# Up products of a SwiGLU trunk made token by token, with eleven pairs of weight pieces multiplied in seven quarter products instead of eight

## The chip, the core and the metric

The kernel runs on one core of a Trainium2 chip. The engines are named as in the profile: PE multiplies matrices (PEld is its loading of the stationary operand), DVE and ACT work element by element, POOL does small work on statistics, and SP issues the DMA transfers. The metric is the device time of one execution in microseconds (us); the median of several runs is compared.

## What is computed

Two layers of a decoder trunk for 256 tokens of 1024 features, everything in float32. Each layer is a half-step SwiGLU, a token mixer beside a memory attention, and a second half-step SwiGLU:

```python
def swiglu(h, w_up, w_down):
    gate, up = jnp.split(h @ w_up, 2, axis=-1)
    return (jax.nn.silu(gate) * up) @ w_down

x = x + 0.5 * swiglu(rmsnorm(x, norm_g[i, 0]), ffn_w_up[i, 0], ffn_w_down[i, 0])
h = rmsnorm(x, norm_g[i, 1])
# mixer: multi-scale causal pooling in layer 0, differential attention in layer 1
x = x + mix
x = x + 0.5 * swiglu(rmsnorm(x, norm_g[i, 2]), ffn_w_up[i, 1], ffn_w_down[i, 1])
```

The change lies in the four SwiGLUs. `w_up` is 1024 x 5632 (gate and up of 2816 each), `w_down` is 2816 x 1024.

## The kernel before, in words

**Float32 in two parts.** Every operand of a product is split exactly into two float32r parts, hi and lo. ACT makes hi by a cast, DVE makes lo by a subtraction, and a product is hi·hi + hi·lo + lo·hi, added up in PSUM. The weights stream from HBM in pieces of 128 x 2048 numbers (1 MB). One DMA on SP loads a piece into one of three raw buffers, four casts and four subtractions of 512 columns split it (L196 to L210), and at most four split pieces are alive (`WB = 4`); a fifth waits until PE has read the oldest.

**One SwiGLU.** `ffn` (L401) goes over eleven column blocks j. A block's up weights are two pieces (upper and lower half of the 1024 rows, each with 256 gate and 256 up columns), its down weights are one piece.
- The first block (three in the first SwiGLU) is made *token by token*: `proj_tok` (L344) keeps 128 tokens stationary and streams 512 weight columns, three matmuls of 512 columns (`mm3`, L230) for each of eight K tiles. Then `gated` takes silu on ACT and the product with the up half on DVE, and PE transposes the result, since the down product needs features on the partitions.
- The other blocks are made *wide*, feature by feature: `proj_wide` (L368) keeps 128 x 128 weights stationary and streams the hi and lo columns of all tokens side by side, one matmul of 512 columns and one of 256 for each K tile. Nothing has to be transposed. ACT and DVE add the two halves of the bank, multiply by the row of token norms, take silu and multiply.
- The down product of a block (`accumulate`, L387) adds 24 matmuls of 512 columns to four PSUM banks.

At the end of a SwiGLU or a mixer, `close` (L293) transposes the new x on PE, and ACT and DVE write its columns, times the gain, into `xT` as hi and lo. The norm of a token (`rstd`) is made meanwhile on ACT and POOL, and comes in only after the up product.

**What sets the order.** `Flow` (L63) writes the instructions of PE, ACT, DVE and SP in an order that it plans by hand-set spacings: products form the main stream, and the steps of chains (split a piece, gate a block, close a tile) are laid between them. Each engine then works strictly down its list: an instruction that waits holds all that stand behind it.

## Time and profile before

| | |
|---|---|
| median of 3 runs | 1035.28 us (1034.5 to 1036.14) |
| span of the profiled execution | 1033.5 us |
| PE busy | 99% of the span |
| DVE busy | 72% |
| ACT busy | 59% |
| granted clock of PE | 0.998 on the mean |

The profile page gives the busy time of each engine, the span in 40 slices, the chain of work that ended last, and the costliest groups of instructions. In a row of a group, "418" is the mean time of one in ns; the start of the next one can lie before the reported end of the last, since the engines are pipelined. The span goes from the first to the last instruction; the 1.8 us that the median is longer lie around it.

### The profile page before, as it was taken

How to read it: one execution, taken by the hardware profiler on the slowest of the kernel's cores; microseconds unless marked ns; L12 is line 12 of the kernel's file. 1: busy time of each engine (PE TensorE's matmuls, PEld its weight loads, DVE VectorE, ACT ScalarE, POOL GpSimd, SP SyncE). 2: the span in 40 equal slices, each digit the busy share in tenths (PEclk: the TensorE clock that was granted, in tenths of full speed). 3: DMA queues.
4: the chain of work that ended last, by engine and by line, in shares of the span. 5: the costliest groups of instructions: out<-in, count | busy, mean ns of one | idle time of the engine just before them, and what ended most of it. 6: DMA issues, size and time to landing. Idle time of an engine off the chain costs nothing.

```text
span 1033.5 us, 15028 instructions
## 1 busy us (share of the span) xinstructions
PE 1022.4 (99%) x5624; PEld 882.0 (85%) x5624; DVE 739.6 (72%) x1533; ACT 610.4 (59%) x1357; POOL 55.8 (5%) x125
## 2 busy tenths in 40 slices
PE   8999999999999999999999999999999999999997
PEld 7888888899888888888888888889998888888886
DVE  5767887756767677777777777756877867777675
ACT  5655755765666555556655565654766666555553
POOL 0000520100000000000000000010211000000000
PEclk9999999999999999999999999999999999999999
DMA  8754745535544555544554545446334544455541
GB/s 300 286 189 163 267 181 204 201 130 188 182 140 168 192 199 193 200 170 163 204 202 165 204 163 204 169 157 237 120 134 142 185 158 168 164 203 178 195 178 41
DMA packets 27993, 188.31 MB, mean 182 GB/s; under 512 B 3216, under 2 KB 3472, under 8 KB 5904
## 3 DMA queue, kind: packets, MB, share of 16 engines
q1 hardware_dynamic: 27632, 186.82, 49.7%
q8 instruction: 44, 0.72, 0.3%
q10 hardware_dynamic: 288, 0.52, 0.1%
q14 instruction: 29, 0.24, 0.1%
HBM read 186.29 MB, written 1.05 MB: 181 GB/s over the span
## 4 chain that ended last, share of the span: by engine, by line
PE 95%; DVE 2%; ACT 1%; DMA 1%; POOL 0%; SPq 0%; issue 0%; POOLq 0%; ACTq 0%
PE mm L377 28%; PE mm L379 12%; PE acc L231 10%; PE acc L233 10%; PE acc L232 10%; PE mm L231 6%; PE mm L233 6%; PE mm L232 6%; PE mm L376 2%; PE tr L237 1%; DMA raw<-in_ffn_w_up 1%; DVE lo L208 1%; ACT ds L841 1%; PE acc L822 0%; PE tr L232 0%; PE tr L233 0%
## 5 line engine op out<-in xcount | busy, mean ns | idle before, releaser
L208 DVE TENSOR_TENSOR lo<-raw,hi 128x512 fp32r<-128x512 f32 x684 | 440.7, 688 | 43.0 <-ACT hi L205 42.7
L377 PE MATMUL mm<-xT,hi 128*128 128x512 f32 x1216 | 424.2, 398 | 0.0
L205 ACT CAST hi<-raw 128x512 fp32r<-128x512 f32 x684 | 385.1, 618 | 26.9 <-PE mm L232 14.2
L379 PE MATMUL mm<-xT,lo 128*128 128x256 f32 x1064 | 298.5, 281 | 0.0
L377 PEld LDWEIGHTS mm<-xT,hi 128*128 128x128 f32 x1216 | 220.8, 188 | 42.4
L379 PEld LDWEIGHTS mm<-xT,lo 128*128 128x128 f32 x1064 | 201.0, 189 | 6.4
L231 PE MATMUL acc<-hi,gh 128*128 128x512 f32 x352 | 138.1, 392 | 0.0
L233 PE MATMUL acc<-hi,gl 128*128 128x512 f32 x352 | 137.1, 389 | 0.0
L232 PE MATMUL acc<-lo,gh 128*128 128x512 f32 x352 | 137.0, 389 | 0.0
L385 DVE TENSOR_TENSOR g<-g,mm 128x256 f32<-128x256 f32 x76 | 32.0, 421 | 80.6 <-ACT g L384 80.4
L384 ACT COPY s<-mm 128x256 f32<-128x256 f32 x76 | 28.3, 372 | 98.7 <-PE mm L377 98.7
L232 PEld LDWEIGHTS acc<-lo,gh 128*128 128x128 f32 x352 | 66.2, 188 | 13.9
L233 PEld LDWEIGHTS acc<-hi,gl 128*128 128x128 f32 x352 | 66.1, 188 | 14.0
L231 PEld LDWEIGHTS acc<-hi,gh 128*128 128x128 f32 x352 | 66.1, 188 | 11.9
L385 DVE TENSOR_TENSOR s<-s,mm 128x256 f32<-128x256 f32 x76 | 31.9, 420 | 57.8 <-ACT s L384 57.7
L439 ACT ACTIVATE s<-s 128x256 f32<-128x256 f32 x76 | 31.8, 418 | 68.5 <-DVE s L437 68.5
L220 ACT CAST gh<-g 128x256 fp32r<-128x256 f32 x76 | 30.9, 407 | 65.8 <-DVE g L445 65.8
L231 PE MATMUL mm<-xT,hi 128*128 128x256 f32 x192 | 55.9, 291 | 0.0
L233 PE MATMUL mm<-xT,lo 128*128 128x256 f32 x192 | 54.5, 284 | 0.0
L232 PE MATMUL mm<-xT,hi 128*128 128x256 f32 x192 | 54.3, 283 | 0.0
L231 PE MATMUL mm<-hi,xT 128*128 128x512 f32 x128 | 50.9, 398 | 0.0
L233 PE MATMUL mm<-hi,xT 128*128 128x512 f32 x128 | 50.0, 390 | 0.0
(190 smaller groups left out, 1364.1 us busy)
## 6 DMA issues: line engine op xcount, KB each, us to landing
raw<-in_ffn_w_up SPq DMA_DIRECT2D x86, 1024.0 KB, 4.8
raw<-in_ffn_w_down SPq DMA_DIRECT2D x44, 1024.0 KB, 5.0
raw<-in_diff_w_in SPq DMA_DIRECT2D x14, 1024.0 KB, 4.8
raw<-in_mem_w_kv SPq DMA_DIRECT2D x8, 1024.0 KB, 4.8
raw<-in_pool_w_in SPq DMA_DIRECT2D x6, 1024.0 KB, 4.9
raw<-in_pool_w_out SPq DMA_DIRECT2D x6, 1024.0 KB, 4.8
raw<-in_diff_w_out SPq DMA_DIRECT2D x6, 1024.0 KB, 4.7
raw<-in_ffn_w_up SPq DMA_DIRECT2D x8, 256.0 KB, 7.0
```

Source lines behind the costliest of these rows:

```text
L205: nc.scalar.copy(hi[:, sl], raw[:, sl])
L208: nc.vector.tensor_sub(lo[:, sl], raw[:, sl], hi[:, sl].bitcast(F32))
L220: nc.scalar.copy(hi, src)
L231: nc.tensor.matmul(o, lh, rh, start=start, stop=False)
L232: nc.tensor.matmul(o, lh, rl, start=False, stop=False)
L233: nc.tensor.matmul(o, ll, rh, start=False, stop=stop)
L376: nc.tensor.matmul(o[:, 0:SEQ], wl, hx[0][:, kk, :], start=False, stop=False)
L377: nc.tensor.matmul(o, wh, hx[2][:, kk, :], start=kk == 0, stop=last)
L379: nc.tensor.matmul(o[:, 0:SEQ], wl, hx[0][:, kk, :], start=False, stop=False)
L384: nc.scalar.copy(out, o[:, SEQ:2 * SEQ])
L385: nc.vector.tensor_add(out, out, o[:, 0:SEQ])
L439: nc.scalar.activation(s, s, AF.Silu)
```

## The change

All blocks of a SwiGLU are made token by token; `proj_wide` and its helpers are gone. Up blocks are either *single* (as `proj_tok` before) or taken in *pairs* of two blocks, two pairs in the first SwiGLU and three in each of the others. A pair is a product of a 2 x 2 matrix of operand quarters (two tiles of 128 tokens, two halves of K) and a 2 x 2 matrix of weight pieces (two halves of K, two blocks): eight quarter products before, seven now. Each quarter product is four `mm3`, twelve matmuls of 512 columns. They are made in the order 1, 5, 6, then the down product of an earlier block, then 2, 7, 3, 4.

For this the pair needs sums. Of the weights: piece 5 is b11 + b12, piece 6 adds b22 to that, piece 4 is b21 plus all the others, and piece 7 is b12 + b22. (The signs of the scheme sit in the sums of the operand and in the order of subtraction.) DVE makes these in float32 in place in the raw buffers, eight additions of 128 x 1024, and all seven pieces are split into hi and lo. Pieces b12 and b22 are loaded into the room of the mixers' tiles (`qk`, `mq`). Of the operand: `column_sums`, once for each SwiGLU, multiplies the float32 columns by the row of norms and makes five sums of 128 x 512, each split.

The seven results are put together by DVE (`less`, `gate_sum`): u2 = result 6 − m1 where m1 is result 1 copied out by ACT, then product 7 is added to the same bank and u3 = that − m1, u2 += result 3, u3 += m5, c21 = m1 − result 4. Each of the four quarters is then gated (silu on ACT, product on DVE) and transposed on PE, two transposes for each quarter and block.

Other edits: a split works in halves of 1024 columns instead of quarters of 512; `close` first writes the scaled columns in float32 and then casts them, four activations and one cast on ACT and one subtraction on DVE where there were four and four; the weight queue counts free buffers by kind; the condition that queues the memory's columns and statistics in the first SwiGLU now holds at two of its steps, so that they are loaded and made twice.

```diff
-SPLIT = 512
+SPLIT = 1024
+PAIR = (0.15, 0.9, 0.55, 0.75)
+PAIR_SLACK = 3.0
...
     def split_piece(key, raw, before):
...
+        for s in range(0, PIECE, SPLIT):
+            sl = slice(s, s + SPLIT)
+            if before is not None:
+                nc.vector.tensor_add(raw[:, sl], raw[:, sl], before[:, sl])
+            nc.scalar.copy(hi[:, sl], raw[:, sl])
+            yield pace
+        for s in range(0, PIECE, SPLIT):
+            sl = slice(s, s + SPLIT)
+            nc.vector.tensor_sub(lo[:, sl], raw[:, sl], hi[:, sl].bitcast(F32))
...
     def close(t, gain0, xg):
...
+            for k in range(4):
+                g = gain0 + 4 * h + k
+                nc.scalar.activation(c[:, k, :], b[h][:, cols(k)], AF.Copy, scale=gcol[:, g:g + 1])
+            b[h] = c
+            split_hi(xT[0][:, 4 * h:4 * h + 4, cols(t)], c)
...
+    def column_sums(xg):
...
+        row = row_rstd(rstd)
+        yield 0.6
+        nc.vector.tensor_mul(xg, xg, row.unsqueeze(1).to_broadcast([P, KT, SEQ]))
...
+            nc.vector.tensor_sub(v, in0, in1)
+            if made:
+                finish_last()
+            split_hi(hi[:, i], v)
...
+        def columns_of(js, t, made):
+            F.finish(*made)
+            yield PAIR_SLACK
...
+            for i, j in enumerate(js):
+                transposes(b[:, cols2(i)], gts[j, t], 2)
...
+        def pair(a, between):
...
+            product(1, first, *plain(0), True)
+            m1 = F.add(keep("m1", first, rstd[0]))
+            product(5, second, *summed(0), True)
+            m5 = F.add(keep("m5", second))
+            product(6, third, *summed(1), True)
+            F.finish(m1)
+            u2 = F.add(less("u2", third, kept["m1"]))
+            between()
+            product(2, first, *plain(1), False)
+            c11 = F.add(gate_first())
+            F.finish(u2)
+            product(7, third, *summed(2), False)
+            u3 = F.add(less("u3", third, kept["m1"]))
+            F.finish(m5)
+            product(3, second, *summed(3), False)
+            c12 = F.add(gate_sum(js[1], 0, "u2", second))
+            F.finish(u3)
+            ids[js[0], 0] = ids[js[1], 0] = F.add(columns_of(js, 0, (c11, c12)))
+            c22 = F.add(gate_sum(js[1], 1, "u3", kept["m5"]))
+            product(4, third, *summed(4), False)
+            c21 = F.add(gate_less())
+            ids[js[0], 1] = ids[js[1], 1] = F.add(columns_of(js, 1, (c22, c21)))
...
+    def steps(begin):
+        if begin:
+            return [("single", 1), ("single", 2), ("down", 0, 1), ("pair", 3, 2), ("single", 5), ("down", 3, 4),
+                    ("pair", 6, 5), ("single", 8), ("down", 6, 7), ("single", 9), ("down", 8), ("single", 10),
+                    ("down", 9, 10)]
+        return [("single", 0), ("pair", 1, 0), ("single", 3), ("down", 1, 2), ("pair", 4, 3), ("single", 6),
+                ("down", 4, 5), ("pair", 7, 6), ("single", 9), ("down", 7, 8), ("single", 10), ("down", 9, 10)]
...
+            W.add(b11, up[layer, f, a, 0], frees=())
+            W.add(b12, up[layer, f, a + 1, 0], "qk", HOLD_PIECE)
+            W.add(key + (5,), None, pre=plus(b11, b12), frees=())
+            W.add(b22, up[layer, f, a + 1, 1], "mq", HOLD_PIECE)
+            W.add(key + (6,), None, pre=plus(b11, b22), frees=())
+            downs(*between)
+            W.add(b21, up[layer, f, a, 1], post=all_four)
+            W.add(key + (7,), None, pre=plus(b12, b22), frees=("qk",))
+            W.add(key + (3,), None, pre=lambda raw: (raw[b22], None), frees=("mq",))
+            W.add(key + (4,), None, pre=lambda raw: (raw[b21], None))
```

**Place 1: DVE in the middle of a round.** Before, in the second SwiGLU, a block's splits (L208) stand with the few steps that join the halves of a wide tile (L385 to L445):

```order
L208 TENSOR_TENSOR lo_469_3453<-raw_457_3339,hi_468_3452 128x512 x4
L385 TENSOR_TENSOR s_472_3460<-s_472_3460,mm_474_3462 128x256
L437 TENSOR_TENSOR s_472_3460<-s_472_3460,row_426_3135 128x256
L208 TENSOR_TENSOR lo_478_3496<-raw_463_3390,hi_477_3495 128x512 x2
L385 TENSOR_TENSOR g_473_3461<-g_473_3461,mm_475_3485 128x256
L444 TENSOR_TENSOR g_473_3461<-g_473_3461,row_426_3135 128x256
L445 TENSOR_TENSOR g_473_3461<-g_473_3461,s_472_3460 128x256
L208 TENSOR_TENSOR lo_478_3496<-raw_463_3390,hi_477_3495 128x512
L226 TENSOR_TENSOR gl_471_3459<-g_473_3461,gh_470_3458 128x256
```

Now, in the second pair of the same SwiGLU, from the step after product 6 (bank tr_528) on. hi_534/lo_535 is piece 2, 538/539 piece 7, 540/541 piece 3, 545/546 piece 4; mm_526 is the bank of products 1 and 2, mm_527 that of 5 and 3:

```order
L572 TENSOR_TENSOR u2_536_3291<-tr_528_3233,m1_529_3234 128x512
L248 TENSOR_TENSOR lo_535_3268<-raw_508_3101,hi_534_3267 128x1024
L1134 TENSOR_TENSOR raw_508_3101<-raw_508_3101,raw_496_3042 128x1024 x2
L243 TENSOR_TENSOR raw_497_3044<-raw_497_3044,raw_498_3046 128x1024 x2
L248 TENSOR_TENSOR lo_539_3311<-raw_497_3044,hi_538_3310 128x1024 x2
L491 SCALAR_TENSOR_TENSOR g_542_3342<-mm_526_3231,rstd_431_2693,s_543_3346 128x256
L248 TENSOR_TENSOR lo_541_3337<-raw_498_3046,hi_540_3336 128x1024
L572 TENSOR_TENSOR u3_544_3360<-tr_528_3233,m1_529_3234 128x512
L248 TENSOR_TENSOR lo_541_3337<-raw_498_3046,hi_540_3336 128x1024
L248 TENSOR_TENSOR lo_546_3367<-raw_508_3101,hi_545_3366 128x1024
L583 TENSOR_TENSOR u2_536_3291<-u2_536_3291,mm_527_3232 128x512
L248 TENSOR_TENSOR lo_546_3367<-raw_508_3101,hi_545_3366 128x1024
```

Moved: additions of raw pieces have come in, and steps that read a finished product now stand between the two halves of a piece that a coming product needs.

**Place 2: the end of a pair, on DVE and PE.** Before, PE goes from one tile of a block straight to the next, with no transpose:

```order
L379 MATMUL mm_474_3462<-xT_95,lo_466_3414 128x256
L376 MATMUL mm_474_3462<-xT_95,lo_466_3414 128x256
L377 MATMUL mm_474_3462<-xT_95,hi_465_3413 128x512
L377 MATMUL mm_475_3485<-xT_95,hi_458_3341 128x512
L379 MATMUL mm_475_3485<-xT_95,lo_459_3342 128x256
```

Now PE has one `mm3` of the next single block (piece hi_548/lo_549) between the last matmul of product 4 and the transposes of c21 and u3:

```order
L275 MATMUL tr_528_3233<-hi_545_3366,sum_lo_453_2824 128x512
L273 MATMUL mm_565_3441<-hi_548_3384,xT_95 128x512
L274 MATMUL mm_565_3441<-lo_549_3385,xT_95 128x512
L275 MATMUL mm_565_3441<-hi_548_3384,xT_95 128x512
L279 MATMUL tr_568_3448<-ident_83,c21_562_3431 128x128 x2
L279 MATMUL tr_568_3448<-ident_83,u3_544_3360 128x128 x2
```

and on DVE this stands between the last row of place 1 and the gated c21:

```order
L489 TENSOR_TENSOR u2_536_3291<-u2_536_3291,s_550_3387 128x256
L583 TENSOR_TENSOR u3_544_3360<-u3_544_3360,m5_530_3235 128x512
L248 TENSOR_TENSOR lo_549_3385<-raw_514_3132,hi_548_3384 128x1024
L489 TENSOR_TENSOR u3_544_3360<-u3_544_3360,s_556_3407 128x256
L267 TENSOR_TENSOR gl_552_3399<-tr_555_3402,gh_551_3398 128x2x128
L267 TENSOR_TENSOR gl_554_3401<-tr_555_3402,gh_553_3400 128x2x128
L248 TENSOR_TENSOR lo_549_3385<-raw_514_3132,hi_548_3384 128x1024
L572 TENSOR_TENSOR c21_562_3431<-m1_529_3234,tr_528_3233 128x512
L489 TENSOR_TENSOR c21_562_3431<-c21_562_3431,s_563_3434 128x256
```

Moved: PE's next product has a transpose in it that waits for the last row of this list. (The gated u2 is transposed in the middle of product 4.)

**Place 3: DVE at the start of the second SwiGLU.** Before, behind the first block's gate:

```order
L416 SCALAR_TENSOR_TENSOR g_419_3099<-mm_407_3025,rstd_402_2994,s_418_3098 128x256
L260 COPY row_426_3135<-tr_425_3132 128x256
L416 SCALAR_TENSOR_TENSOR g_422_3128<-mm_420_3100,rstd_416_3093,s_421_3127 128x256
L208 TENSOR_TENSOR lo_424_3130<-raw_396_2936,hi_423_3129 128x512 x4
L385 TENSOR_TENSOR s_429_3139<-s_429_3139,mm_431_3141 128x256
```

Now, in the same place (raw_388/lo_450 is piece 6, sum_454 and sum_lo_453 are sums of the operand):

```order
L491 SCALAR_TENSOR_TENSOR g_443_2781<-mm_434_2718,rstd_431_2693,s_445_2786 128x256
L302 COPY row_447_2804<-tr_446_2801 128x256
L385 TENSOR_TENSOR xg_425_2657<-xg_425_2657,row_447_2804 128x2048
L243 TENSOR_TENSOR raw_388_2443<-raw_388_2443,raw_421_2621 128x1024
L402 TENSOR_TENSOR sum_454_2825<-xg_425_2657 128x512
L491 SCALAR_TENSOR_TENSOR g_448_2816<-mm_444_2782,rstd_442_2778,s_451_2821 128x256
L402 TENSOR_TENSOR sum_455_2829<-xg_425_2657,sum_454_2825 128x512
L267 TENSOR_TENSOR sum_lo_453_2824<-sum_454_2825,sum_hi_452_2823 128x512
L243 TENSOR_TENSOR raw_388_2443<-raw_388_2443,raw_421_2621 128x1024
```

Moved: the sums of the operand and the additions of piece 6 share DVE's list with the gate of the block that runs meanwhile.

## Rows read from the trace of the kernel before

**Rows 1.** The page: busy us (share of the span) and instructions; clock by slice

```profile
PE 1022.4 (99%) x5624; PEld 882.0 (85%) x5624; DVE 739.6 (72%) x1533; ACT 610.4 (59%) x1357; POOL 55.8 (5%) x125
PEclk9999999999999999999999999999999999999999
```

**Rows 2.** What PE waited for: us in total, times, longest

```profile
PE acc L231 <- ACT xT L222: 2.0, 2, 1.5
PE tr L237 <- DVE on L876: 1.2, 3, 0.6
```

**Rows 3.** One round of a wide block: span, busy us and instructions, clock, DMA

```profile
352.92:369.64 16.72, 16.72 (x90) 14.32 (x89) 12.16 (x24) 9.47 (x20) 0.00 (x0) 1.00 0.51 190
```

**Rows 4.** The chain that ended last: starts of wide tiles; transposes in fours

```profile
310.13 0.44 PE tr L237 x4
...
336.20 0.47 PE mm L377 x2
339.02 0.47 PE mm L377 x2
```

**Rows 5.** Timeline of PE: the first of a down product's 24 matmuls, and the first behind them

```profile
344.73 0.40 PE L231 MATMUL acc<-hi,gh 128*128 128x512 f32 x1
...
350.18 0.39 PE L377 MATMUL mm<-xT,hi 128*128 128x512 f32 x1
```

**Rows 6.** Timeline of DVE: splits in a row, with the steps beside them

```profile
363.92 0.42 DVE L226 TENSOR_TENSOR gl<-g,gh 128x256 fp32r<-128x256 f32 x1
364.25 4.30 DVE L208 TENSOR_TENSOR lo<-raw,hi 128x512 fp32r<-128x512 f32 x7
370.31 0.42 DVE L385 TENSOR_TENSOR s<-s,mm 128x256 f32<-128x256 f32 x1 [1.76 <-ACT s L384]
370.77 0.42 DVE L437 TENSOR_TENSOR s<-s,row 128x256 f32<-128x256 f32 x1
```

**Rows 7.** Groups: shapes, count, busy us, mean ns, idle before

```profile
L228 DVE SCALAR_TENSOR_TENSOR memT<-raw,gcol,memT 128x256 fp32r<-128x256 f32 x8 | 3.3, 477 | 0.0
L439 ACT ACTIVATE s<-s 128x256 f32<-128x256 f32 x76 | 31.8, 418 | 68.5 <-DVE s L437 68.5
```

**Rows 8.** Timeline of ACT: casts in a row, and the end of a tile

```profile
363.75 3.22 ACT L205 CAST hi<-raw 128x512 fp32r<-128x512 f32 x6
...
369.91 0.37 ACT L384 COPY s<-mm 128x256 f32<-128x256 f32 x1 [2.15 <-PE mm L377]
```

**Rows 9.** Timeline of PE at that tile's end

```profile
369.48 0.63 PE L377 MATMUL mm<-xT,hi 128*128 128x512 f32 x2
```

**Rows 10.** Start of the second SwiGLU on PE: first product, transposes of x, next product

```profile
304.06 0.39 PE L231 MATMUL mm<-hi,xT 128*128 128x512 f32 x1
...
308.14 0.60 PE L237 MATMUL tr<-ident,x_res 128*128 128x128 f32 x4
...
310.33 0.48 PE L231 MATMUL mm<-hi,xT 128*128 128x512 f32 x1
```

**Rows 11.** The same stretch on ACT: columns of x, statistics, table, silu

```profile
308.78 1.14 ACT L222 ACTIVATE xT<-tr,gcol 128x128 fp32r<-128x128 f32 x4 [1.63 <-PE tr L237]
...
312.57 0.21 ACT L251 ACTIVATION_READ_ACCUMULATOR junk<-x_res 128x1 f32 x1
312.80 1.28 ACT L414 ACT_TABLE_LOAD   x1
314.10 0.47 ACT L414 ACTIVATE s<-mm,rstd 128x256 f32<-128x256 f32 x1
```

**Rows 12.** The same stretch on DVE: the gate's product

```profile
314.61 0.48 DVE L416 SCALAR_TENSOR_TENSOR g<-mm,rstd,s 128x256 f32<-128x256 f32 x1 [1.69 <-ACT s L414]
```

**Rows 13.** Start of the program on PE, at its slow clock and after

```profile
7.45 0.63 PE L233 MATMUL acc<-hi,xT 128*128 128x512 f32 x1
7.88 0.63 PE L231 MATMUL acc<-hi,xT 128*128 128x512 f32 x1
```

**Rows 14.** DMA issues on SP: count, KB each, median us to landing

```profile
raw<-in_ffn_w_up SPq DMA_DIRECT2D x86, 1024.0 KB, 4.8
```

More of the change, by code (lines that the diff above doesn't have):

```diff
@@ new lines, in plan_ffn @@
+        for kind, *js in steps(begin):
+            if kind == "pair":
+                pair(*js)
+            elif kind == "down":
+                downs(*js)
+            else:
+                for q in range(2):
+                    W.add((layer, f, "up", js[0], q), up[layer, f, js[0], q])
+            if begin and kind == "single" and js[0] == 2:
+                W.add("x", I["x"].rearrange("b (t p) d -> p (b t) d", p=P), "none")
+            if begin and js[-1] == 5:
+                W.add("cols", I["mem_cols"])
+                W.add("mem", I["mem"].rearrange("b (t p) d -> p (b t) d", p=P))
```

447 lines of the change are left out of this document (267 added, 180 removed).

## The prediction

> **What bounds the kernel now.** I read the page first: PE is busy 99% of the span, DVE 72%, ACT 59%, and the clock stands at 9 in all forty slices [rows 1]. Then what PE waited for: the largest item is 2.0 us in two waits, the largest on DVE 1.2 us in three [rows 2]. So before the change nothing but PE's own work sets the time, and each later operand arrives in time. The windows view of one round says with what margin: in 16.72 us PE works throughout, DVE 12.16, ACT 9.47, the DMA engines half of the time [rows 3]. DVE has 4.6 us of slack in a round. That slack is what the change spends.
>
> **Prices.** A wide tile takes 339.02 − 336.20 = 2.82 [rows 4], so a wide block 4 × 2.82 = 11.28. The 24 matmuls of a down product take 350.18 − 344.73 = 5.45 [rows 5], or 0.227 each; 11.28 + 5.45 is the round of 16.72 again. A token-major block is 48 such matmuls: 10.90. A quarter product is 12: 2.72. Four transposes take 0.44 [rows 4].
> For DVE I use distances of starts. Seven subtractions of 512 columns take 4.30 reported [rows 6]; the report of the last is some 0.08 longer than its slot (a 256-column step shows 0.42, the next starts 0.33 later), so 0.60 each, 0.33 for 256 columns. The 256 columns more cost 0.27, so 1024 cost an estimated 0.60 + 2 × 0.27 = 1.14 and 2048 cost 2.2. A step that needs the one just before it starts 0.46 after it, 0.13 later than in a free list [rows 6]. A step with three operands takes 0.41 (3.3 busy for eight), a silu 0.42 on ACT [rows 7]. A cast of 512 takes 0.54 [rows 8], so 1024 about 1.0. Handoffs: the last matmul of a tile starts at 369.48 and, at 0.227, hands its slot on at 369.71 [rows 9]; ACT starts at 369.91 [rows 8], 0.2 later; DVE starts 0.03 after ACT's reported end [rows 6].
>
> **PE's arithmetic.** Before, 38 of the 44 blocks are wide. Made token-major each saves 0.38 and pays 0.44 for transposes: 38 × 0.06 = +2.3. Each of the eleven pairs drops one quarter product: 11 × 2.72 = −30.0. Net −27.7. If nothing ever waited: 1033.5 − 27.7 = 1005.8 span, and with the 1.8 around it 1007.6; the profiled execution plus 1.8 is the median, so I carry the difference over as it is.
> The Trainium skill (TensorE: Matmul & The Clock Gate, section Back-to-back issue gap) gives N/2.4 + 2.5 ns for one matmul, 215.8 ns at 512 columns. By that figure, an estimate, a quarter product would be 2.59 and eleven 28.5 instead of 30.0. The trace's 227 decides.
>
> **DVE's arithmetic.** A round of a pair and a single block replaces three rounds. PE: 3 × 16.35 − 2.72 + 3 × 0.44 = 47.6, before 3 × 16.72 = 50.2. DVE: twelve pieces (seven of the pair, two of the single block, three of down weights) in halves, 24 × 1.14 = 27.4; eight additions, 9.1; five 512-column steps, 3.0; gates and the low parts of their results, 4.1; together 43.6, before 3 × 12.16 = 36.5. DVE goes from 73% to 92% of the round. On the mean it would still fit. But its list is fixed, and work that depends on PE sits at a few places of it.
>
> **The tail of a steady pair.** Take t = 0 at the end of product 6. DVE's first step there, u2, needs that product, so nothing of the following can be done ahead. Up to the gated c21 its list (the change's places 1 and 2) holds 13 steps of 1024 columns (14.8), five of 512 (3.0), five of 256 (1.7) and one gate (0.4): 19.9 us. PE's list up to the transposes of c21 is the down product 5.45, four quarter products 10.9, four transposes 0.44, one mm3 0.68: 17.45. So DVE alone is 2.6 late with the first handoff of 0.2, without a single wait of its own. It does wait: replaying the list with the prices above, 0.24 for c11's silu, 0.7 at u3 (product 7 ends at 10.89, DVE stands there at 10.5), 0.3 at u2 (product 3), 0.6 at c21 for its own silu. Gated c21 is ready at about 21.9, so 4.4 are lost: 0.46 where product 3 wants the second low half of its piece, 0.8 at the transposes of u2, 3.15 at those of c21. The low bound takes only the latency chains, DVE at leisure: product 4's end to gated c21 is 0.2 + 0.6 + 0.13 + 0.42 + 0.33 with two short handoffs, 1.8, against 0.68 of cover, so 1.1; the like at u2 gives 0.9; together 2.0. The high bound is 5.5, with each of the waits falling on PE in full. Eight pairs run so (the second and third of the three later SwiGLUs, both of the first): 8 × 4.4 = **35.2**, between 16 and 44.
>
> **The first pair of a later SwiGLU.** Product 5 comes 15.7 us after the first matmul of the opening block and needs the operand's sums. Before, that block's opening runs from 304.06 over the transposes of x at 308.14 to 310.33 [rows 10]; the statistics are read at 312.57, the table is loaded until 314.08, the silu runs at 314.10 [rows 11], DVE's gate at 314.61 [rows 12]: 10.5 after the start. Now two casts stand ahead of the statistics, about 1.0 later, and behind the gate DVE has the row's copy 0.33, the multiplication of all columns 2.2, an addition 1.14 and the first sum 0.6, then ACT a cast. With the queue on ACT the first sum's hi comes at 17.65 and its lo at 18.85: 2.7 us of waiting for product 5. Behind it product 6 waits 2.2 for its low part, since DVE is still at the sums; the down product waits 3.1 for the opening block's columns, whose cast stands on ACT behind four large casts; the tail gives 4. That is 12; the low bound, the sums alone and the tail's 2.0, is 5; the high one 14. Some of it may be made up in the waits ahead, so I take 10: 3 × 10 = **30**.
>
> **The rest.** At five closings one cast more on ACT lies before the first product of what follows: between 0 and 1.0 each, 0.6 taken, **3**. In the first SwiGLU the memory's columns are made twice: 8 × 0.41 = 3.3 on DVE [rows 7], in a pair's tail, with nothing behind which to hide; and its sums are about 1 late: **4**. The longer table of loads costs nothing: a piece lands 4.8 us after its issue [rows 14], and the pieces held in the mixers' rooms only change which buffer is filled. Sum: 35.2 + 30 + 3 + 4 = 72.2 of waits; 1035.3 − 27.7 + 72.2 = **1080**. With the bounds of the first two terms: 1050 (16 + 21 + 5) to 1103.
>
> **Rivals.**
> 1. *Latency alone.* DVE gets ahead where I have it late, because the 1024-column steps cost less than my estimate. Then 8 × 2.0 + 3 × 5 − 27.7, with 1 of smaller items left, is +4: 1039. With none of the sums' wait it is 1030, with 10 of smaller items 1048. Against it: the 2.6 us of plain DVE work in each tail.
> 2. *The other side: DVE keeps up.* The waits at c21 and at the sums would have to be at most 1 us a pair, because the steps of a tail are shorter by a fifth (13 steps of 1024 at 0.9 give 16.8, under PE's 17.45). It decides at about 27.7/11 = 2.5 us lost per pair: below that the change is faster. Full gain 1007; with 1 us a pair 1018. For it: the mean fits (43.6 in 47.6). Against it: no row has a 512-column step under 0.6.
> 3. *PE's clock falls.* Waits of 3 us stand where there were none. At the slow clock a matmul of 512 columns takes 0.43, from 7.45 to 7.88 [rows 13], against 0.227; that is the lower level, 1.2 for 2.4 GHz, before PE had worked for long. If each of 11 to 19 waits made one quarter product run slow, 12 × 0.2 = 2.4 each adds 26 to 46: 1105 to 1125. The Trainium skill (TensorE: Matmul & The Clock Gate, section Why this matters for your kernels) says that idle gaps between bursts of matmuls send the clock back to half; in the trace of before the waits are at most 1.5 us and the clock keeps its level [rows 1, 2], so no run here has tried it.
> 4. *That the change does not do what it says* (a product not dropped): PE's matmuls are counted in the order of its instructions, seven times twelve for each pair, so I leave it out.
>
> **How the numbers follow.** Forecast 0.62, at 1080 with 1050 to 1103. Latency alone 0.16: 0.03 of it faster, 0.03 the same, 0.10 slower. DVE keeps up 0.14, all faster. Clock 0.08, slower. Faster 0.17, same 0.03, slower 0.80, where 0.2% is about what a measurement of this kernel can tell from no change. The range goes from 1015, which leaves out half of the second rival, to 1103, which leaves out the third: 0.15 outside.
>
> **What would show it.** Among PE's waits one on DVE before the transposes of c21, about 3 us, in nearly every pair, and a smaller one at u2; product 5 of each later SwiGLU's first pair waiting 2 to 3 us for a sum; 27 to 28 us less of PE's work proper; DVE without idle time from u2 to c21; a round of pair and single at about 52 us. I am wrong if the 1024-column steps start less than 1.0 apart, if DVE stands idle before c21 while PE does not wait, or if the granted clock leaves its level.

## The result: 10.7% slower

The changed kernel takes 1145.61 us (median of 4 runs, 1144.5 to 1146.9), the kernel before beside it 1034.89: a ratio of 1.1071, 95% interval 1.1055 to 1.1087. Slower was right; 1080 was not, nor was the range up to 1103. Of the 110 us that the profiled execution is longer, the prediction had 45.

The page, first line and clock, of the changed kernel; they answer to [rows 1]:

```profile
PE 1045.4 (91%) x5040; PEld 859.8 (75%) x5040; DVE 825.2 (72%) x1069; ACT 625.2 (55%) x987; POOL 74.5 (7%) x137
PEclk9999989999998999999999999989999999998999
```

PE now stands still for about a tenth of the span, and in four slices of forty the clock is below 9. What PE waited for (us in total, times, longest), the first five rows; [rows 2] had 2.0 at the head:

```profile
PE tr L279 <- DVE c L489: 29.1, 10, 2.9
PE acc L273 <- ACT gh L261: 12.1, 7, 2.3
PE tr L279 <- DVE u L489: 9.2, 11, 3.8
PE tr L274 <- DVE lo L248: 6.6, 9, 1.5
PE mm L273 <- ACT xT L261: 6.4, 3, 2.1
```

The windows view by stage, cut at the last transposes of each closing (span, then busy us of PE, PEld, DVE, ACT and POOL, then the clock): first SwiGLU, mixer, second and third SwiGLU, mixer, fourth.

```profile
0.00:225.68 225.68, 203.69 (x876) 162.41 (x877) 166.30 (x198) 130.16 (x193) 44.91 (x74) 0.96 0.56 207
225.68:340.60 114.92, 110.96 (x642) 98.16 (x640) 67.43 (x99) 60.83 (x105) 4.34 (x10) 0.99 0.48 172
340.60:552.11 211.51, 191.15 (x822) 152.82 (x821) 163.13 (x182) 114.40 (x160) 1.48 (x4) 0.96 0.44 164
552.11:766.69 214.58, 192.45 (x821) 153.68 (x820) 163.25 (x181) 116.40 (x166) 2.77 (x5) 0.95 0.41 154
766.69:933.95 167.26, 164.22 (x1102) 146.83 (x1101) 108.77 (x236) 96.20 (x218) 18.28 (x37) 1.00 0.45 162
933.95:1143.90 209.95, 182.88 (x785) 145.86 (x783) 156.32 (x177) 107.21 (x150) 2.73 (x8) 0.96 0.37 138
```

Before, the same cuts gave 201.0, 109.0, 186.2, 186.3, 164.6 and 186.4, all at a clock of 0.99 or 1.00. So the SwiGLUs lose 24 to 28 each, and the mixers, in which no product was changed, 6.0 and 2.6. The clock is low chiefly where SwiGLUs run.

To split the 110, I took the distances between the starts of PE's instructions in both traces, less the prices of the prediction (0.227 for 512 columns and so on), and put what is over 0.25 down as a wait, and stretches in which neighbouring matmuls take nearly double as slow clock:

| | us |
|---|---|
| PE's own work, by those prices | −27.7 |
| waits: 106.4, before 4.8 | +101.6 |
| matmuls at the slow clock: 28.8, before 3.2 | +25.6 |
| the rest, delays under 0.25 among them (by difference) | +11 |
| sum | +110.4 |

And the waits by place, beside the prediction:

| place | predicted | in the trace |
|---|---|---|
| tails of pairs: c21 30.7, u2 11.0, product 3's low part 3.9 | 47 | 45.6 |
| first pair of a later SwiGLU: products 5 and 6, first down product | 18 to 24 | 20.1 |
| closings | 3 | 6.9 |
| the rest of the first SwiGLU | 4 | 9.5 |
| ends of the SwiGLUs: the last down product waits for its own block | 0 | 10.7 |
| mixers | 0 | 7.6 |

Left out are 2.8 at the program's start, about as before, and 3.0 of first slow matmuls right behind a wait. One wait at u2, of 4.0, holds 3.2 that belong to the memory's columns: their eight steps (3.25 of DVE) stand in that tail, as the prediction's last term had it.

One wait at c21 and what comes behind it, on PE (start, reported duration):

```profile
491.59 0.40 PE L275 MATMUL mm<-hi,xT 128*128 128x512 f32 x1
494.92 0.41 PE L279 MATMUL tr<-ident,c 128*128 128x128 f32 x2 [2.93 <-DVE c L489]
...
496.22 0.63 PE L273 MATMUL mm<-hi,xT 128*128 128x512 f32 x1
496.65 0.63 PE L274 MATMUL mm<-lo,xT 128*128 128x512 f32 x1
...
498.78 0.63 PE L273 MATMUL mm<-hi,xT 128*128 128x512 f32 x1
499.21 0.43 PE L274 MATMUL mm<-lo,xT 128*128 128x512 f32 x1
499.48 0.40 PE L275 MATMUL mm<-hi,xT 128*128 128x512 f32 x1
```

From 491.59 + 0.23 to 494.92 are the 3.1 us of the prediction. Then, from 496.22 to 499.21, seven matmuls stand 0.43 apart, as in [rows 13] and not as in [rows 5]: the clock is at its lower level, 1.2 GHz, and then comes back by itself.

DVE's list ahead of that c21, from u2's sum with product 3 on:

```profile
487.24 0.69 DVE L583 TENSOR_TENSOR u<-u,mm 128x512 f32<-128x512 f32 x1 [0.38 <-PE mm L275]
487.84 1.22 DVE L248 TENSOR_TENSOR lo<-raw,hi 128x1024 fp32r<-128x1024 f32 x1
488.98 0.42 DVE L489 TENSOR_TENSOR u<-u,s 128x256 f32<-128x256 f32 x1
489.31 0.68 DVE L583 TENSOR_TENSOR u<-u,m 128x512 f32<-128x512 f32 x1
489.91 1.22 DVE L248 TENSOR_TENSOR lo<-raw,hi 128x1024 fp32r<-128x1024 f32 x1
491.05 0.42 DVE L489 TENSOR_TENSOR u<-u,s 128x256 f32<-128x256 f32 x1
491.38 0.75 DVE L267 TENSOR_TENSOR gl<-tr,gh 128x256 fp32r<-128x256 f32 x2
492.05 1.21 DVE L248 TENSOR_TENSOR lo<-raw,hi 128x1024 fp32r<-128x1024 f32 x1
493.18 0.68 DVE L572 TENSOR_TENSOR c<-m,tr 128x512 f32<-128x512 f32 x1
494.34 0.42 DVE L489 TENSOR_TENSOR c<-c,s 128x256 f32<-128x256 f32 x1 [0.48 <-ACT s L484]
```

The 1024-column steps start 1.13 to 1.14 after one another; the estimate of [rows 6] held. What is to be seen at the first row is the 0.38: DVE waited for product 3 there.

### The profile page after: what moved, and what is told of

It is laid out like the page before. It is cut to its first block, busy times and chain, and to the rows that moved or that the text cites. A ratio compares the mean times of both kernels' runs of the same rounds, so it can differ in the third digit from the quotient of the medians.

```text
span 1143.9 us, 13127 instructions
## 1 busy us (share of the span) xinstructions
PE 1045.4 (91%) x5040; PEld 859.8 (75%) x5040; DVE 825.2 (72%) x1069; ACT 625.2 (55%) x987; POOL 74.5 (7%) x137
## 4 chain that ended last, share of the span: by engine, by line
PE 67%; DVE 19%; ACT 7%; issue 3%; DMA 2%; POOL 1%; SPq 0%; POOLq 0%; ACTq 0%; DVEq 0%
PE mm L274 12%; PE mm L275 12%; PE mm L273 11%; DVE lo L248 8%; PE acc L275 8%; PE acc L273 8%; PE acc L274 8%; ACT hi L244 2%; PE tr L279 2%; DVE raw L243 2%; PE tr L274 2%; PE tr L275 2%; PE tr L273 2%; DMA raw<-in_ffn_w_up 1%; DVE u L583 1%
## 5 line engine op out<-in xcount | busy, mean ns | idle before, releaser
L244 ACT CAST hi<-raw 128x1024 fp32r<-128x1024 f32 x408 | 412.1, 1048 | 232.3 <-DVE raw L243 79.6
L248 DVE TENSOR_TENSOR lo<-raw,hi 128x1024 fp32r<-128x1024 f32 x408 | 484.3, 1223 | 28.7 <-ACT hi L244 27.8
L273 PE MATMUL mm<-hi,xT 128*128 128x512 f32 x472 | 192.8, 408 | 6.4 <-ACT xT L261 6.4
L275 PE MATMUL mm<-hi,xT 128*128 128x512 f32 x472 | 189.6, 402 | 0.0
L274 PE MATMUL mm<-lo,xT 128*128 128x512 f32 x472 | 189.4, 401 | 0.0
L273 PE MATMUL acc<-hi,gh 128*128 128x512 f32 x352 | 143.7, 408 | 12.5 <-ACT gh L261 12.1
L273 PEld LDWEIGHTS mm<-hi,xT 128*128 128x128 f32 x472 | 92.5, 196 | 25.9 <-ACT xT L261 7.1
L275 PEld LDWEIGHTS mm<-hi,xT 128*128 128x128 f32 x472 | 92.0, 195 | 21.2 <-DVE xT L267 1.3
L274 PEld LDWEIGHTS mm<-lo,xT 128*128 128x128 f32 x472 | 92.3, 196 | 19.4
L243 DVE TENSOR_TENSOR raw<-raw,raw 128x1024 f32<-128x1024 f32 x66 | 78.0, 1217 | 0.0
L274 PE MATMUL tr<-lo,sum_hi 128*128 128x512 f32 x132 | 52.8, 400 | 6.6 <-DVE lo L248 6.6
L273 PE MATMUL mm<-xT,hi 128*128 128x256 f32 x192 | 56.1, 292 | 1.1 <-DVE mq L267 1.1
L275 PE MATMUL mm<-xT,lo 128*128 128x256 f32 x192 | 54.5, 284 | 0.2 <-DVE lo L248 0.2
```

The source lines that it names most:

```text
L243: nc.vector.tensor_add(raw[:, sl], raw[:, sl], before[:, sl])
L244: nc.scalar.copy(hi[:, sl], raw[:, sl])
L248: nc.vector.tensor_sub(lo[:, sl], raw[:, sl], hi[:, sl].bitcast(F32))
L273: nc.tensor.matmul(o, lh, rh, start=start, stop=False, skip_group_check=more)
L274: nc.tensor.matmul(o, lh, rl, start=False, stop=False, skip_group_check=more)
L275: nc.tensor.matmul(o, ll, rh, start=False, stop=stop, skip_group_check=more)
```

## The experiments

All times are medians; the kernel before, run on the same chip, took 1034.5 to 1036.1.

**1. Does a wait of PE by itself slow its clock?** In the kernel before, a made wait ahead of seven down products in each of the last three SwiGLUs, nothing else changed (the diffs from here on are cut):

```diff
+        def idle(n):
+            b = tr_bank()
+            transposes(b, ident, 1)
+            v = t2k("s")[:, 0:P]
+            nc.vector.tensor_copy(v, b[:, 0:P])
+            for _ in range(n):
+                nc.vector.tensor_copy(v, v)
+            transposes(b, v, 1)
...
         def down(j, t, end=None):
...
+            if t == 0 and 2 <= j <= 8 and begin is None:
+                idle({(0, 1): 1, (1, 0): 5, (1, 1): 9}[layer, f])
```

> The kernel before, with a made wait of PE ahead of seven down products in the second, third and fourth SwiGLU: a transpose, a chain of dependent small copies on DVE (1, 5, 9 behind the first copy), and a transpose of their result. DVE's backlog comes on top, so the waits are about 0.7 to 3, 2 to 4 and 3 to 6 us. Theory (a wait of PE of about 3 us by itself brings its clock down for the some 4 us that follow): after waits of 3 us and more the next matmuls take 0.43 for some 8 to 10 of them, 1.7 to 2 us lost, after waits up to 1.5 us none; mean clock falls by SwiGLU from 1.00 to about 0.95. Rival (the clock falls for what DVE and PE do together in the quarter products, or over the whole run): all matmuls at 0.227, clock 1.00 in all three, only the idle time is added.

Measured: 1090.0 (1.0525, 1.0494 to 1.0556). DVE had no backlog in these places, so the waits are 0.81, 1.86 and 2.90 us by SwiGLU, seven of each. The windows of the three SwiGLUs, then the PE timeline at one of the waits of 2.90 and at one of 1.86:

```profile
310.05:504.15 194.10, 189.58 (x991) 160.08 (x990) 140.31 (x291) 110.27 (x236) 2.30 (x4) 1.00 0.49 179
504.15:705.53 201.38, 189.54 (x991) 160.08 (x990) 146.70 (x319) 110.37 (x237) 3.10 (x5) 1.00 0.47 173
870.17:1087.80 217.63, 191.60 (x955) 160.71 (x953) 145.84 (x329) 101.80 (x216) 2.75 (x8) 0.95 0.38 141
```

```profile
924.65 0.33 PE L237 MATMUL tr<-ident,s 128*128 128x128 f32 x1 [2.74 <-DVE s L460]
924.73 0.62 PE L231 MATMUL acc<-hi,gh 128*128 128x512 f32 x1
925.15 0.63 PE L232 MATMUL acc<-lo,gh 128*128 128x512 f32 x1
...
593.37 0.27 PE L237 MATMUL tr<-ident 128*128 128x128 f32 x1
595.34 0.33 PE L237 MATMUL tr<-ident,s 128*128 128x128 f32 x1 [1.69 <-DVE s L460]
...
595.97 0.40 PE L233 MATMUL acc<-hi,gl 128*128 128x512 f32 x1
596.20 0.40 PE L231 MATMUL acc<-hi,gh 128*128 128x512 f32 x1
```

Behind the fourteen waits of 0.81 and 1.86 the clock holds at 1.00. Behind five of the seven of 2.90 the next 6 to 14 matmuls of 512 columns take 0.43 (924.73 to 925.15), 1.3 to 2.9 us lost each time. So a wait alone can do it, with no quarter product in sight. In the changed kernel a slow stretch follows seven of the ten c21 waits; these seven lose some 13 of the 25.6. Most of the others stand behind shorter waits that come close together: in seven of the eight places of that trace where a wait of 1.8 to 2.5 us and one of 0.5 to 1.2 start within 3 us of one another, 5 to 12 matmuls are slow behind them (0.88 at 533.48 and 1.78 at 535.82, then eight). Behind the three waits of 2.29 at closings, each by itself, there are none. So no single length of wait parts the two cases in these traces.

**2. Is c21 late for DVE's work?** The changed kernel without the additions of weight pieces, so that pieces 4 to 7 are split as they were loaded:

```diff
-            if before is not None:
-                nc.vector.tensor_add(raw[:, sl], raw[:, sl], before[:, sl])
...
-                    sl = slice(s, s + SPLIT)
-                    nc.vector.tensor_add(raw[b21][:, sl], raw[b21][:, sl], raw[b11][:, sl])
                     yield PACE
```

> The changed kernel without the additions of weight pieces (pieces 5, 6, 7 and 4 are split as they were loaded; the sums of the weights are left out of the computation). Theory (DVE's work between product 6 and the gated c21 is 19.9 us against 17.45 of PE, so it is DVE's load): the tail falls to 15.3, the 3.1 us at c21 fall to about 1.1 (its own latency), the small waits for lo in product 3 go, 3.9 in all, and most of the slow clock behind c21, 1.7 each: 1095 to 1105, clock 0.98 or more. Rival (the wait at c21 is the latency of its chain in the list, whatever stands ahead): 3.0 at c21 as now, over 1135.

Measured: 1123.0 (1.0843, 1.0812 to 1.0875). The wait at c21 is the same to a hundredth. Its row among PE's waits, then DVE's timeline in a tail:

```profile
PE tr L277 <- DVE c L487: 29.1, 10, 2.9
```

```profile
475.73 0.48 DVE L489 SCALAR_TENSOR_TENSOR g<-mm,rstd,s 128x256 f32<-128x256 f32 x1 [4.57 <-ACT s L484]
...
481.28 0.69 DVE L581 TENSOR_TENSOR u<-u,mm 128x512 f32<-128x512 f32 x1 [0.38 <-PE mm L273]
...
487.23 0.68 DVE L570 TENSOR_TENSOR c<-m,tr 128x512 f32<-128x512 f32 x1
488.39 0.43 DVE L487 TENSOR_TENSOR c<-c,s 128x256 f32<-128x256 f32 x1 [0.48 <-ACT s L482]
```

DVE stands idle for 4.57 us ahead of c11's gate, which is the four additions, and comes to u2's sum with the same wait of 0.38 for product 3. From there to the gate of c21 it takes 488.39 − 481.28 = 7.11; in the changed kernel 494.34 − 487.24 = 7.10. The time lies between what theory and rival had (1095 to 1105, over 1135), but the wait at c21 decides for the rival: what makes c21 late is not the sum of DVE's work but the part of its list that stands behind its last wait for PE. The 22 us that this kernel is shorter come from the low parts and the sums, which DVE reaches earlier: 15.6 of waits, 4.8 of slow clock.

**3. Can PE wait later instead?** Both pairs of transposes 3 us further down PE's list, then only those of c21 and u3:

```diff
-PAIR_SLACK = 3.0
+PAIR_SLACK = 6.0
```

> PAIR_SLACK 6.0 instead of 3.0: PE's transposes of a pair's gated quarters stand 3 us (four or five mm3) further down its list, nothing else moves. Theory (the lateness is local, and the following single block, with 8.3 us of DVE work in 16 of PE, makes it up): the 10 waits of 3.1 at c21 and the 11 of about 1 at u2 go, and the slow clock behind c21 with them, about 1.7 each; what stands behind stays: 1144 - 31 - 10 - 16 = 1085 to 1095, clock 0.98. Rival (DVE is late as a whole): the waits come back later in the list, at lo or at the next down product, over 1125.

```diff
-            yield PAIR_SLACK
+            yield PAIR_SLACK if t == 0 else 6.0
```

> Only the second transposes of a pair (c21 and u3) stand 3 us later in PE's list, behind about five mm3 of the next single block; those of u2 stay. Theory (what is late at c21 is the part of DVE's list behind its last wait for PE, u2's sum with product 3: 7.5 us of steps up to the gated c21, against 4.6 of PE; once a wait re-anchors the list, what stood ahead of it doesn't count, and the bank of the u2 transposes is free by then, unlike with both moved): the ten waits of 3.1 go, and the slow clock behind them, 1.7 to 2.5 each; the u2 waits of 0.8 stay: 1145 - 31 - 18 = 1092 to 1102, clock 0.98. Rival (DVE is late as a whole, and the wait comes back at the low parts of the next pieces, as it did with both moved): 1125 to 1135.

Measured: 1132.2 (1.0932, 1.0868 to 1.0996) and 1118.7 (1.0806, 1.0774 to 1.0837). The head of PE's waits, of the first and of the second:

```profile
PE tr L279 <- DVE gl L267: 17.9, 11, 2.1
```

```profile
PE mm L274 <- DVE lo L248: 14.8, 25, 1.0
```

With both moved, the c21 transposes wait for gl: the one bank that both pairs of transposes use is not read yet, a wait of 2.2 in place of one of 3.1 in most pairs; the rival's time (over 1125) came. With c21 alone, its 30.7 us are gone and the slow clock falls from 28.8 to 17.7, but the low parts of the next single block come up with some 14 that they didn't have: half of the rival was right. 27 of the expected 43 to 53 are gained.

**4. What do the blocks cost without pairs?** Eleven single blocks, down products one block behind, no sums; the memory's columns made once:

```diff
-        return [("single", 0), ("pair", 1, 0), ("single", 3), ("down", 1, 2), ("pair", 4, 3), ("single", 6),
-                ("down", 4, 5), ("pair", 7, 6), ("single", 9), ("down", 7, 8), ("single", 10), ("down", 9, 10)]
...
+            out = [("single", 0), ("single", 1), ("down", 0), ("single", 2), ("down", 1), ("single", 3), ("down", 2)]
+        for j in range(4, NJ):
+            out += [("single", j), ("down", j - 1)] if j < NJ - 1 else [("single", j), ("down", j - 1, j)]
```

> No pairs: all eleven blocks of each SwiGLU single and token-major, down products one block behind, no sums of weights or of the operand; the other edits (splits of 1024 columns, the closing with its cast) stay. Theory (the change's time is mostly the pairs' waits and the slow clock behind them, but the end of each SwiGLU costs by itself): PE's work +2.3 against before, at each of four SwiGLU ends the last block's transposes stand directly ahead of its down product, 3 to 3.6 us of waiting each and about 1.7 us of slow clock behind it, at five closings about 1: 1052 to 1060, clock 0.99. Rival (only the pairs cost anything): 1037 to 1040, no wait above 1.5 us.

Measured: 1069.9 (1.0331, 1.0301 to 1.0361), above both. Of the 35, 21 are waits and some 7 slow clock; of the waits the ends of the SwiGLUs have 11, and the first mixer is 7 longer. Then the splits in quarters again, in two ways:

```diff
-SPLIT = 1024
-PACE = 1.2
-HURRY = 0.8
+SPLIT = 512
+PACE = 0.0016
+HURRY = 0.0016
```

> No pairs as in no_pairs, and the splits again in quarters of 512 columns at the pace of the kernel before. Theory (of the 34 us that the kernel without pairs is longer, about 9 in the mixers and some 8 in the first SwiGLU come from the splits in large halves: a wait for a small step behind a 1.1 us one, and both casts before the first subtraction; the ends of the SwiGLUs, 12 and some slow clock, do not): 1050 to 1056; mixers as before, 109 and 164.6. Rival (the mixers' and the first SwiGLU's loss is from the closing's cast or the memory's columns): 1066 to 1070, mixers 115 and 167.

Measured: 1082.9 (1.046, 1.0418 to 1.0503), worse. The edit doesn't do what its expectation says: the number was per column before and is per step here, so all eight steps of a piece came at once and stood ahead of small steps on both engines. It tells nothing of the size. The second way:

```diff
+            for s in range(0, PIECE + 512, 512):
+                if s < PIECE:
+                    sl = slice(s, s + 512)
+                    nc.scalar.copy(hi[:, sl], raw[:, sl])
+                if s:
+                    sl = slice(s - 512, s)
+                    nc.vector.tensor_sub(lo[:, sl], raw[:, sl], hi[:, sl].bitcast(F32))
+                yield 0.0016 * 512
+            return hi, lo
```

> No pairs, and the splits as in the kernel before: quarters of 512, each subtraction one step behind its cast, 0.82 planned per step (the earlier run with quarters put all eight steps of a piece at once, which is another order). Theory (the 34 us of the kernel without pairs are: 9 in the mixers and part of the first SwiGLU from the large halves, 12 with 8 of slow clock from the SwiGLUs' ends, 2 of PE's work): mixers 109 to 110 and 164 to 166, SwiGLU ends unchanged, 1050 to 1060. Rival (the closing's cast and the banks that are no longer taken in turn by the mixers make the loss): 1066 to 1072, mixers 115 and 167.

Measured: 1060.1 (1.0231, 1.0202 to 1.0261). The first mixer with large halves, with quarters, and PE's longest item with quarters:

```profile
210.88:326.91 116.03, 112.08 (x641) 99.29 (x640) 67.52 (x98) 62.78 (x111) 4.34 (x10) 0.97 0.44 155
```

```profile
210.57:319.55 108.98, 108.98 (x642) 96.67 (x641) 69.91 (x132) 65.69 (x145) 3.28 (x9) 1.00 0.48 167
```

```profile
PE acc L283 <- ACT gh L271: 8.2, 4, 3.0
```

The mixer is back at 109.0, so its loss came with the large halves and their order in the lists (both changed here, so no run parts the two). Its largest wait has a longer chain than a small step behind a large one. In the changed kernel's timeline, SP, POOL, DVE and PE:

```profile
252.34 0.33 SPq L230 DMA_DIRECT2D raw<-in_mem_w_kv  x1
252.72 0.42 SPq L963 DMA_DIRECT2D lp<-in_diff_lambda  x1
257.59 0.59 POOL L969 TENSOR_TENSOR pr<-lp 128x64 f32<-128x64 f32 x2 [27.18 <-DMA lp<-in_diff_lambda]
258.22 0.29 DVE L971 TENSOR_REDUCE dots<-pr 128x2 f32<-128x128 f32 x1 [5.95 <-POOL pr L969]
259.16 0.38 PE L274 MATMUL tr<-pl,hi 128*128 128x256 f32 x1 [3.93 <-DVE pl L267]
```

A small load (`lp`, constants of the second mixer) now stands on SP behind a weight load that waits for its raw buffer until 252.3. It lands 4.8 us later; DVE waits 5.95 for the step on POOL that needs it, and behind that stands the low part that PE waits for. In the kernel before, the same load is issued at 216.74, ahead of that weight load at 227.72, and DVE doesn't wait for it. DVE's wait is 5.9 in the kernel without pairs and 0.2 with quarters in turn. The second mixer's 2.6 were not followed.

Of the 25 us that are left, 11 are waits at the ends of the SwiGLUs, where the last block's transposes stand directly ahead of its down product; splitting in quarters didn't touch them.

**5. Pairs later, the last block's transposes earlier.** Two single blocks ahead of the first pair of a later SwiGLU, one down product between the last single block and its own:

```diff
...
+        return [("single", 0), ("single", 1), ("down", 0), ("pair", 2, 1), ("single", 4), ("down", 2, 3),
+                ("pair", 5, 4), ("single", 7), ("down", 5, 6), ("pair", 8, 7), ("single", 10), ("down", 8),
+                ("down", 9, 10)]
...
-            yield SLACK
+            yield SLACK if j < NJ - 1 else 3.0
```

> The steps in another order: in the later SwiGLUs two single blocks ahead of the first pair instead of one (pairs 2, 5 and 8 in place of 1, 4 and 7), one down product between the last single block and its own, whose transposes come 4.3 us earlier; in the first SwiGLU the last downs one block further behind. Nothing is left out. Theory (product 5 waits for sums that are ready 18.9 us after the opening, and the last block's down product for its own transposes): the 3 x 6.5 us at the first pairs' products 5, 6 and first down product go, and the 11 at the SwiGLUs' ends with about 2 of slow clock at each of seven places: 1145 - 19 - 11 - 14 = 1098 to 1110. Rival (these waits move to the tails of the pairs, as DVE has as much to do): over 1125.

Measured: 1106.8 (1.0691, 1.0644 to 1.0738), as the theory had it. The 12.1 for gh are gone from PE's waits, and the product that waited for sums is never late.

**6. All of it together, by steps.** If places in the lists are the cause and not DVE's load, then a kernel with the same products and sums must come down to the kernel before or below it. Each step took the waits that the trace of the last one still showed.

> The edits of late_c21 and of later_pairs together, and the memory's columns loaded and made once. Theory (waits and the slow clock add up by place): 1145 - 49 - 44 - 4 = 1045 to 1062, clock 0.99. Rival (DVE's load of 92% of a round lets the late places come back elsewhere): 1080 to 1110.

The edits of late_c21 and later_pairs, the memory's columns once: 1078.2 (1.0414, 1.0384 to 1.0444), better than its rival's 1080 but 16 above the theory. Left were waits of 0.5 to 1.2 us for low parts. So in quarter products and in the first tile of a single block the matmuls that need only high parts go first:

```diff
-                    mm3(bank, sh[:, k, :], sl[:, k, :], wh[:, k, :], wl[:, k, :], start and k == 0, k == 3, not start)
...
+                    nc.tensor.matmul(bank, sh[:, k, :], wh[:, k, :], start=start and k == 0, stop=False,
+                                     skip_group_check=not start)
+                    nc.tensor.matmul(bank, sl[:, k, :], wh[:, k, :], start=False, stop=False,
+                                     skip_group_check=not start)
...
+                for k in range(4):
+                    nc.tensor.matmul(bank, sh[:, k, :], wl[:, k, :], start=False, stop=k == 3,
+                                     skip_group_check=not start)
```

> best1, and in a quarter product and in the first tile of a single block the matmuls that need only the weights' high parts first (four or eight K tiles), those with the low parts behind; the u2 transposes 1.2 us later; the last block's transposes 1.5 us earlier. Nothing is left out. Theory (what is left in best1 are waits of 0.5 to 1.2 us of a matmul for a low part, 30 us in all, and 9 at u2, which are short lateness against DVE's list and go when PE's list has other work to do there): 1078 - 25 - 8 - 4 = 1038 to 1048. Rival (DVE is late as a whole): 1060 or more, other waits on DVE instead.

1055.2 (1.0184, 1.0154 to 1.0214): 23 gained, between theory and rival, the clock back at 0.998. From here spacings move, and the mixers' pieces are again split in quarters in turn.

> best2, with the pieces planned 0.95 instead of 1.2 us per step in the SwiGLUs, so that DVE's list has a coming piece's halves about one piece earlier, and the mixers' pieces split as in the kernel before. Theory (lateness is a matter of the place in the list): another 6 to 9 in the mixers and 3 to 8 in the SwiGLUs: 1023 to 1038. Rival (what is brought forward makes DVE's steps on products later, u2 and c21): 1040 to 1060.

1053.6 (1.0169, 1.0139 to 1.0198): the mixers' 8.5 came back, the SwiGLUs lost as much at c21 and at the bank of the first pair's product 7; the rival.

> best2, with the mixers' pieces split as in the kernel before, the transposes of u2 0.3 us and those of c21 2 us later, and the first block's transposes 3.3 us earlier in the later SwiGLUs. Theory (places): the mixers return to 109 and 164.7 (8.5 less), the waits at c21 go (7) and half of those at the first down products (3), the lo waits in the rounds stay: 1034 to 1042. Rival (DVE's load): c21's wait turns into longer lo waits, 1045 or more.

1045.9 (1.0103, 1.0074 to 1.0133): c21's waits are gone, and those for the low parts of single blocks have grown from 6 to 12.5, the rival.

> best4 with pieces planned 0.95 us per step. Theory (places): the lo waits go as well, c21's 12 us of best3 go, the 2.1 at the fourth product of a first pair stay: 1033 to 1041. Rival (load): 1045 or more.

1037.9 (1.0028, 1.0014 to 1.0042), within the theory.

> best4 with pieces planned 1.08 us per step. Theory (places): between the two in what is brought forward, with few lo waits and without the wait in first pairs: 1028 to 1036. Rival (load): 1045 or more.

1041.0 (1.0068, 1.0045 to 1.0092), between the two, with one wait of 1.06 left in every round, at u2.

> best6 with the transposes of u2 1.7 us later, those of c21 0.7 later and the first block's 1.5 earlier. Theory (places): the one wait left in every round, 1.06 to 1.65 us at u2, goes, 13 in all, and one of the three at the openings: 1041 - 14 = 1024 to 1030. Rival (DVE's load of 92% in a round is the bound): the wait turns up at c21, at a low part or at the bank of the transposes, 1036 or more.

1036.3 (1.0015, 1.0005 to 1.0025). It lands on the rival's 1036, but its trace has no new wait of that size: u2's fell only to 0.6 in most rounds, and the first SwiGLU lost 3 us more at the memory's statistics and the first transposes. (The execution that was traced took 1040.9, the longest of its ten.)

> best7 with pieces planned 1.02 instead of 1.08 us per step. Theory (places): as best7 or 1 to 3 better, since a few low parts come earlier, unless the bank wait of first pairs (2.1 us in four places at 0.95) comes back: 1022 to 1032. Rival (load): 1036 or more.

1040.9 (1.0049, 1.0032 to 1.0065): bringing the splits forward again gained nothing; the rival.

> best7, with the memory's columns and statistics made beside single block 9 of the first SwiGLU instead of in a pair's tail, the first blocks' transposes there 1 to 4 us later, and the transposes of u2 and c21 0.8 us later. Theory (places): the waits of 3.3, 3.6 and 1.3 in the first SwiGLU go with 1.5 of slow clock, and the 0.6 to 1.2 at u2 in each round: 1036 - 10 - 7 = 1017 to 1026, faster than the kernel before. Rival (DVE's load): other waits come up in their place, 1032 or more.

1034.5 (0.9996, 0.9987 to 1.0005), the rival's time. The memory's place gained its 5 us; moving the first transposes later made a new wait of 7.3, since the casts that free their bank then stood behind those of the operand's sums on ACT. The last kernel's edits at these places, against the changed kernel:

```diff
-            yield PAIR_SLACK
+            yield 8.5 if t == 0 else 12.0
...
-        sums[0] = F.add(column_sums(xr), 26.0)
+        sums[0] = F.add(column_sums(xr), 36.0)
...
-            if begin and js[-1] == 5:
+            if begin and kind == "single" and js[0] == 9:
```

> best9, with the first blocks' transposes where they were, the operand's sums of the first SwiGLU begun 10 us later (the pair that reads them comes 25 us after), and the transposes of u2 and c21 1.5 and 2 us later. Theory (places): the 7.3 us with 1.2 of slow clock in the first SwiGLU and the 0.6 to 1.2 at u2 in ten rounds go: 1034 - 8 - 7 = 1017 to 1023, faster than the kernel before. Rival (DVE's load of 92% in a round is the bound): waits of that sum come up elsewhere in the rounds, 1030 or more.

**1028.3 us** (5 runs, 1027.62 to 1030.15), a ratio of 0.9936 to the kernel before, 0.9923 to 0.995: 0.6% faster than the kernel before, though short of the 1017 to 1023 expected. So of the ten expectations of this section one theory (1033 to 1041) was met; the rival's time came five times, and the other four lie between. What speaks against the load is the end state. Its first line of the page, the heads of its PE waits, and the window of one round (pair and single block):

```profile
PE 1005.3 (98%) x5036; PEld 841.3 (82%) x5036; DVE 827.7 (80%) x1142; ACT 623.3 (61%) x1057; POOL 71.2 (7%) x133
```

```profile
PE mm L452 <- ACT hi L254: 3.5, 3, 1.2
PE acc L285 <- DVE gl L277: 2.6, 3, 1.1
```

```profile
425.98:473.68 47.70, 47.70 (x217) 39.47 (x216) 44.19 (x50) 28.55 (x37) 0.00 (x0) 1.00 0.50 186
```

In the round PE never waits while DVE is busy 44.2 of 47.7. From one pair's transposes of c21 to the next pair's it is 47.68 to 47.70 in all six steady rounds of the later SwiGLUs, where the prediction had 47.6 for PE alone; in the changed kernel these six took 52.3 to 55.1. DVE's work is about what it was there (827.7 beside 825.2). Its load did not bound these rounds.

## Why the prediction was wrong

**PE's arithmetic** held: the rounds of the last kernel run without a wait in 47.7, and 47.6 was forecast. (The first table can't show it, since its last row is a difference.)

**The tail of a steady pair: right size, wrong reason.** 3.15 at c21 and 0.8 at u2 were forecast, 3.1 and 0.8 measured, because the replay put the last steps in their order. The one of the six steady rounds in which the clock stayed up took 52.3, beside the 47.6 + 4.4 of the replay. But the step "DVE alone is 2.6 late" was no bound: it counted 19.9 us from product 6 on, and DVE waits on the way. The additions can all go (experiment 2) and the wait at c21 stays. The count that decides starts at the last wait of the list for PE, product 3: 7.1 us up to c21's gate. This mattered for the rivals: I held the plain DVE work for the reason against the first one, and in the last kernel the same work makes PE wait nowhere in a round.

**The first pairs** were sized well, 20.1 beside 18 to 24. Product 5 waited 2.0 to 2.5 where 2.7 was forecast.

**The clock** is the largest failure: the sum put it at nothing, and it took 25.6. It stood as a rival with 0.08, 26 to 46 us, on top of the forecast; and the granted clock leaving its level was the prediction's own sign of being wrong. [Rows 1, 2] show waits of at most 1.5 us, and even this one stands at the program's start, where matmuls are still 0.43 apart (6.43, just ahead of [rows 13]); in full stride the longest is 0.6. So nothing of before could say that the clock holds, and I read "no run has tried it" as improbable, though my own forecast put ten waits of 3 us where there were none, and [rows 13] had the price. A consequence of the forecast belongs in its sum. The Trainium skill (TensorE: Matmul & The Clock Gate, section Why this matters for your kernels) warns of just such gaps; the runs agree with it for waits of 2.9 to 3.1 us, in 12 of 17 cases, and did not show it behind single waits of 1.86.

**Terms that were not there.** The ends of the SwiGLUs, 10.7: I priced the order of blocks where it changed in the middle and didn't follow the last one, whose transposes now stand directly ahead of its own down product, where the wide block before had none. The mixers, 7.6: the edit of the split was taken as a DVE saving, and who stands behind a large step was asked only in the SwiGLUs. "The longer table of loads costs nothing" looked at the weight pieces alone; a small load that stood behind one of them cost 4.1 in the first mixer. The closings, 6.9 instead of 3: three waits of 2.29, with two large casts on ACT ahead of the columns of x. The rest of the first SwiGLU, 9.5 instead of 4. And 11 us in delays under a quarter of a microsecond, for which no row of before gave a size and whose parts stay open.

**The range.** Its upper end summed the high bounds of two terms and held all others at about their value. It doesn't even follow from them: 44 + 42 + 7 of waits give 1101, not 1103, and at the lower end three first pairs at 5 are 15, not 21, so 1044, not 1050. With the clock's 26 as a term and the 28 of the missed places the forecast would have been 1133, and most of what is then left is the 11 of small delays.

**Not shown.** Why the clock stays up behind five of the seventeen long waits is open. That the dips of the changed kernel's clock come only from waits follows from experiment 1 by likeness; in late_c21 the waits at c21 go and the slow clock with them (28.8 to 17.7), but other waits come up there, so it isn't shown by itself.

## What to carry to other kernels

On engines that work strictly down a list, find the last step that waits for the critical engine: what stands between it and the step that is waited for is the lateness. Work ahead of it doesn't count as long as the engine still waits there; in the changed kernel that wait was 0.38 us, so little more work would have counted. Here waits of TensorE of about 3 us had slow matmuls behind them in 12 of 17 cases, so a forecast of such waits belongs in the sum together with its price. Look also at the small loads when the order of the large ones moves. A scheme that saves arithmetic pays only when its new steps are placed: nearly the same work took 1146 us in one order and 1028 in another (the memory's columns are made once in the second, and the mixers split in quarters).

## What the runs showed of the hardware

With made waits in the kernel before, PE's clock was at 1.00 behind each of fourteen of 0.81 and 1.86 us, and went to its lower level behind five of seven of 2.90 us, for 6 to 14 matmuls, 1.3 to 2.9 us lost, and then came back while PE worked. A 1024-column subtraction or addition in float32 on DVE starts 1.13 to 1.14 us after the one before it, against 0.60 for 512 columns, so large halves save 5% of a split's time on DVE, and a step behind one of them waits nearly twice as long. A load of 128 KB landed 4.8 us after its issue, as a weight piece of 1 MB does, and it was issued only after the waiting load ahead of it on SP.
